# A hybrid encoder block with product-key expert retrieval on one core: reordered squares, table loads and gelus, narrower lookups, a shared gating product and another end

## Chip, cores and metric

The kernel runs on one core of one Trainium2 chip. The metric is the device time of one execution in microseconds (us); the median of three runs is given.

## What is computed

One layer on x of 512 tokens by 1024, all in float32. `peer` is where most of the time goes: each token picks 16 of 16384 experts for each of 8 heads, and the kernel computes it densely for three of the four blocks of 128 tokens and by gathering rows for the fourth.

```
h    = rms_norm(x, norm1_g)
u_a, v_a, q, k, v = split(h @ w_in)                       # 1024 -> 5 x 512
a_out = spatial_gating(gelu(u_a), gelu(v_a), ...)         # layer norm of v, 8 groups of 128x128
b_out = dilated_attention(rope(q), rope(k), v)            # windows (128,1), (512,4), (2048,16)
x    = x + concat(rms_norm(a_out), rms_norm(b_out)) @ w_out

# peer, on rms_norm(x, norm2_g), for each token and head:
s      = q @ sub_keys                                     # two lists of 128 scores
s1, i1 = top_k(s[0], 16);  s2, i2 = top_k(s[1], 16)
sc, ci = top_k((s1[:, None] + s2[None, :]).reshape(256), 16)
e      = i1[ci // 16] * 128 + i2[ci % 16]
g      = softmax(sc)
act    = gelu(xb @ expert_u[e].T)
x      = x + (g * act) @ expert_v[e]
out    = rms_norm(x, final_norm_g)
```

## The kernel before

The order of the work is written out by hand (`manual_schedule`): each engine does its instructions in the order in which the code issues them. TensorE multiplies float32 numbers as three products of split halves: `split` makes `hi` by a cast on ScalarE (L80) and `lo` by a subtraction on VectorE (L81) or, in some stages, GpSimd (L181), so that each weight tile costs a cast, a subtraction and three times the matmuls.

The stages, by the time of the profiled execution:

- Projections and attention, 0 to 240 us. `proj` multiplies x by pieces of w_in (matmuls L252) into five accumulators, four `acc` and one `pu`. The norm's factor is applied behind the product, so `xsq` makes the sums of squares of the four token blocks in `xss` during the first projection, `inv_root` makes `xrs` of them (a root on ScalarE, L146, and a reciprocal on VectorE), and the scaled copies of q (`qraw`, L270) empty the accumulators for the next projection. A function of ScalarE that its active table doesn't hold needs an ACT_TABLE_LOAD; `warm(f)` (L227) makes a tiny activation to have it early. v is emptied by gelus (`va`, L373).
- Query products and the choice of 16 out of 128, 241 to 346 us, then the rest of the routing up to 401 us: `top16` on VectorE, `decode`, `softmax`. `decode` turns the position ci of a chosen pair into two numbers of 0 to 15 (`rw`, `cl`) and looks the expert's indices up in the two lists: ScalarE spreads `rw` over 16 columns (`oh`, L681), VectorE compares with 0 to 15 (L688), multiplies by the list (L690), and adds the 16 columns pairwise (L695, L697). One call takes the three token blocks of three heads (n = 9 lists of 16 x 16 entries, 2304 numbers) or of two (n = 6). TensorE does the products with the first experts here (`ahead`, L201), up to AHEAD = 31 of 128.
- Gating, 401 to 541 us, 48 steps of 8 tokens. VectorE makes `ohb`, one-hot rows of the second and the first key (L855), and `oha`, the first key's one times the gate in two float16 halves, `gw` (L859); TensorE multiplies them, 16 matmuls of 128 columns (L896), which scatters the gates into a table of 128 x 128 for each token; ScalarE evacuates them into `wst` (`put`, L876), and DMAs on ScalarE's queue store it. `hots` runs two steps ahead of its matmuls. Between them stand 10 product matmuls of `ahead` a step with their casts (`uhi`, L170, and `ulo`, L181), and `flush` has ScalarE's gelus of finished products (`act`, L768).
- The main loop, 541 to 1479 us: e goes over 128 groups of 128 experts. Each e has 24 L201 matmuls (products with expert_u, for a later e, up to e = 96) and 18 L1041 matmuls (`vproduct`: three token blocks b, two halves n of 512 columns, three products hi hi, lo hi, hi lo, which add up in six accumulators over all e). Their inputs are `vhi`, `vlo` (`vsplit`) and `wahi`, `walo` (`wsplit`), for e + 1, made from `vraw`, loaded by SyncE's queue. In the same loop GpSimd gathers expert rows for the fourth token block, and VectorE takes dot products with them (L993) and adds them up (L1002); `rate` spreads these over the loop, and at e = NK - 3 those left are finished.
- The end: sums, gains and norms for the three dense blocks (`final_sum`, `gain`, `root`, `finish`), which begin when a block's accumulators are complete, and four stores.

## Time and profile before

| | |
|---|---|
| median of three runs | 1488.34 us (1487.87 to 1490.42) |
| profiled execution | 1490.96 us |
| its span | 1489.2 us |
| TensorE busy | 1453.4 us, 98% of the span |
| VectorE busy | 1159.6 us, 78% |
| ScalarE busy | 641.3 us, 43% |
| GpSimd busy | 283.6 us, 19% |
| granted TensorE clock, whole span | 0.996 |

The busy shares are means over stages with different limits. A stage has to be read from its own window, and a gap on TensorE from what ended it. PE is TensorE's matmul, PEld its weight load, DVE is VectorE, ACT is ScalarE, POOL is GpSimd, SPq and ACTq are the DMA queues of SyncE and ScalarE. A group xN in a timeline is N instructions in a row of one kind, and its length is the stretch that they take together; brackets give the idle time ahead and what ended it.

### The profile page before, as it was taken

The page shows a single profiled execution, that of the slowest core. Times are in us where ns is not written, and L with a number is a line of the kernel's source. Part 1 is how long each engine was busy: PE and PEld are TensorE (multiplying, and loading weights), DVE is VectorE, ACT ScalarE, POOL GpSimd, SP SyncE. Part 2 cuts the span into 40 slices and gives each one's busy share as a digit, 9 for nine tenths or more (in the row PEclk, how much of TensorE's full clock was granted, in tenths as well). Part 3 has the DMA queues.
Part 4 walks back from the last instruction along what each step waited for, and adds up shares of the span by engine and source line. Part 5 has one row for each costly group of instructions (what it writes and reads, how often), then busy time and mean ns, then how long its engine had stood idle before and what let it go on. Part 6 is the DMA issues. An engine that isn't in the chain of part 4 may idle for free.

```text
span 1489.2 us, 21574 instructions
## 1 busy us (share of the span) xinstructions
PE 1453.4 (98%) x7945; PEld 1292.6 (87%) x7945; DVE 1159.6 (78%) x2415; ACT 641.3 (43%) x1088; POOL 283.6 (19%) x222
## 2 busy tenths in 40 slices
PE   8999999999899999999999999999999999999997
PEld 6878988888888899999999999999999999987785
DVE  4745554999899967779878787888787888877775
ACT  5455753344555544434333333333333333323334
POOL 0040002445500000012222222222222222211002
PEclk9999999999999999999999999999999999999999
DMA  6331032232366776469999999999999998988764
GB/s 217 106 99 57 22 114 104 86 91 96 110 230 256 261 291 214 135 228 378 355 351 329 315 338 321 327 334 336 347 326 333 331 328 308 348 286 299 250 212 160
DMA packets 128777, 358.52 MB, mean 241 GB/s; under 512 B 9120, under 2 KB 59808, under 8 KB 112288
## 3 DMA queue, kind: packets, MB, share of 16 engines
q1 hardware_dynamic: 103184, 197.75, 40.1%
q0 software_dynamic: 18432, 134.23, 23.6%
q10 hardware_dynamic: 7056, 25.18, 4.2%
q8 instruction: 62, 1.02, 0.3%
q14 instruction: 43, 0.35, 0.1%
HBM read 327.10 MB, written 30.02 MB: 240 GB/s over the span
## 4 chain that ended last, share of the span: by engine, by line
PE 78%; DVE 9%; DMA 5%; issue 3%; ACT 3%; POOL 1%; ACTq 0%; SPq 0%; DVEq 0%; POOLq 0%
PE pu L201 34%; PE acc L1041 30%; PE acc L252 6%; DMA vraw<-in_uv_dram 3%; DVE ohb L855 3%; DVE oha L859 2%; DVE ulo L181 1%; DMA uraw<-in_uT_dram 1%; PE tr L734 1%; PE pu L252 1%; PE tr L434 1%; POOL ulo L181 1%; PE acc L447 1%; DVE vlo L81 1%; DMA xt<-in_x_dram 1%
## 5 line engine op out<-in xcount | busy, mean ns | idle before, releaser
L201 PE MATMUL pu<-h2T,uhi 128*128 128x384 f32 (+2 forms) x2336 | 451.0, 342 | 3.2 <-ACT act L768 2.4
L201 PEld LDWEIGHTS pu<-h2T,uhi 128*128 128x128 f32 x2336 | 409.6, 189 | 19.4 <-ACT act L768 3.1
L987 POOL DMA_INDIRECT uv<-in_uv_dram,ei x128 | 170.6, 1333 | 830.1 <-DVE xlast L1002 318.0
L81 DVE TENSOR_TENSOR vlo<-vraw,vhi 128x1024 fp32r<-128x1024 f32 x128 | 156.8, 1225 | 154.9 <-ACT vhi L80 154.7
L80 ACT CAST vhi<-vraw 128x1024 fp32r<-128x1024 f32 x128 | 134.6, 1051 | 296.3 <-issue 188.6
L1041 PE MATMUL acc<-vhi,wahi 128*128 128x512 f32 x768 | 238.7, 391 | 1.9 <-ACT wahi L80 1.9
L1041 PE MATMUL acc<-vlo,wahi 128*128 128x512 f32 x768 | 238.2, 391 | 0.5
L1041 PE MATMUL acc<-vhi,walo 128*128 128x512 f32 x768 | 237.8, 391 | 0.0
L201 PE MATMUL pu<-h2T,ulo 128*128 128x384 f32 (+2 forms) x1168 | 234.1, 340 | 2.3 <-POOL ulo L181 2.3
L201 PEld LDWEIGHTS pu<-h2T,ulo 128*128 128x128 f32 x1168 | 203.7, 188 | 7.4 <-POOL ulo L181 2.9
L170 ACT CAST uhi<-uraw 128x1024 fp32r<-128x1024 f32 x144 | 150.7, 1047 | 61.1 <-DMA uraw<-in_uT_dram 47.6
L1041 PEld LDWEIGHTS acc<-vlo,wahi 128*128 128x128 f32 x768 | 143.8, 188 | 33.7 <-DVE vlo L81 2.4
L1041 PEld LDWEIGHTS acc<-vhi,walo 128*128 128x128 f32 x768 | 143.7, 188 | 31.5 <-DVE walo L81 0.9
L1002 DVE SCALAR_TENSOR_TENSOR xlast<-uv,dot,xlast 128x1024 f32<-128x1024 f32 x128 | 164.5, 1285 | 4.5
L1041 PEld LDWEIGHTS acc<-vhi,wahi 128*128 128x128 f32 x768 | 142.6, 188 | 26.9 <-ACT wahi L80 3.1
L768 ACT ACTIVATE act<-pu 128x384 f32<-128x384 f32 x128 | 62.9, 492 | 234.9 <-PE pu L201 234.5
L993 DVE SCALAR_TENSOR_TENSOR uv<-uv,h 128x1024 f32<-128x1024 f32 x128 | 153.7, 1219 | 6.7 <-DMA uv<-in_uv_dram,ei 6.7
L181 DVE TENSOR_TENSOR ulo<-uraw,uhi 128x1024 fp32r<-128x1024 f32 x116 | 141.5, 1220 | 22.1 <-ACT uhi L170 21.9
L181 POOL TENSOR_TENSOR ulo<-uraw,uhi 128x512 fp32r<-128x512 f32 x56 | 81.5, 1479 | 209.4 <-ACT uhi L170 203.7
L81 DVE TENSOR_TENSOR walo<-wa,wahi 128x384 fp32r<-128x384 f32 x128 | 70.7, 553 | 0.6 <-ACT wahi L80 0.6
L80 ACT CAST wahi<-wa 128x384 fp32r<-128x384 f32 x128 | 65.2, 509 | 13.0 <-DVE wa L1026 12.9
L1026 DVE TENSOR_TENSOR wa<-act,wt 128x384 f32<-128x384 f32 x128 | 70.5, 551 | 0.0
(258 smaller groups left out, 1475.4 us busy)
## 6 DMA issues: line engine op xcount, KB each, us to landing
uraw<-in_uT_dram SPq DMA_DIRECT2D x128, 512.0 KB, 5.9
vraw<-in_uv_dram SPq DMA_DIRECT2D x128, 512.0 KB, 5.3
wd<-wst ACTq DMA_DIRECT2D x48, 512.0 KB, 3.1
wt<-wd SPq DMA_DIRECT2D x32, 768.0 KB, 10.6
wraw<-in_w_in_dram SPq DMA_DIRECT2D x19, 512.0 KB, 3.6
uraw<-in_w_q_dram SPq DMA_DIRECT2D x16, 512.0 KB, 3.8
xT<-in_xT_dram SPq DMA_DIRECT2D x8, 256.0 KB, 3.9
xt<-in_x_dram SPq DMA_DIRECT2D x1, 2048.0 KB, 11.5
```

The costliest lines, as they stand in the source:

```text
L80: S.copy(hi, src)
L81: sub.tensor_tensor(lo, src, hi.bitcast(F32), op=ALU.subtract)
L170: S.copy(hi, raws[i])
L181: eng.tensor_tensor(lo[:, k, :], raws[i][:, k, :], hi[:, k, :].bitcast(F32), op=ALU.subtract)
L201: T.matmul(o, l[:, k, :], r[:, k, t0:n], start=(p == 0 and k == 0), stop=(p == 2 and k == KT - 1))
L252: T.matmul(out[b], l[:, b * 128:(b + 1) * 128], r[:, kk, :], start=(k == 0 and i == 0), stop=(k == KT - 1 and i == 2))
L768: S.activation(acts[e], o[:, :DT], AF.Gelu_apprx_tanh)
L987: G.indirect_dma_start(out=uvs[r].rearrange("p s d -> p (s d)"), out_offset=None, in_=A["uv"], in_offset=bass.IndirectOffsetOnAxis(ap=ei[: ...
L993: V.scalar_tensor_tensor(uv[:, 0, :], uv[:, 0, :], 1.0, h2, op0=ALU.mult, op1=ALU.mult, accum_out=d[:, 0:1])
L1002: V.scalar_tensor_tensor(xlast, uv[:, 1, :], d[:, 1:2], xlast, op0=ALU.mult, op1=ALU.add)
L1026: eng.tensor_tensor(wa.rearrange("p (c t) -> p c t", c=NWC), acts.pop(e).rearrange("p (c t) -> p c t", c=NWC), wts[e // WG][:, :, e % WG, ...
L1041: T.matmul(acc[b][n], l[:, c], r[:, n * 512:(n + 1) * 512], start=(e == 0 and i == 0), stop=(e == NK - 1 and i == 2))
```

## The change

1. At the start `warm` loads the sqrt table in place of the one for Copy, and the squares of the odd token blocks are made on VectorE with an accumulating instruction.
2. The gelu table is loaded before the last head pair's casts of k, and the gelus of v go over the blocks in the order 1, 2, 3, 0.
3. `decode` looks up in 8 columns: 16 rows with the first 8 entries of a list and 8 rows (only those positions that can reach past 8) with the last 8, 192 numbers for a list in place of 256. The comparison table `iota_v` is made by GpSimd, once for each of the two pools.
4. In the gating stage VectorE makes `oha` for seven of eight tokens, and ScalarE the eighth's two halves, by copies scaled with a factor for each partition (`gs`), behind `flush`.
5. The gather's work is spread to end one expert earlier, and the rest is finished at e = NK - 4.
6. The split parts of the last two experts lie in the gather's buffers (`vl`, `wl`), so that those of the four last experts live side by side. Token block 2 of the last four experts (LASTV) is multiplied behind everything else, half n = 0 first, then n = 1.
7. Blocks 0 and 1 are finished with one product of sum, factor and gain on VectorE in halves; the last block's halves are scaled by VectorE and ScalarE and stored from two queues. GpSimd has no gains any more.

```diff
-    warm(AF.Copy)
+    warm(AF.Sqrt)
...
     def xsq(b):
         sq = tk.tile([128, 1024], F32, name="xs", bufs=4)
-        sumsq(sq, xt[:, b, :], xss[:, b:b + 1])
+        if b % 2:
+            V.scalar_tensor_tensor(sq, xt[:, b, :], 1.0, xt[:, b, :], op0=ALU.mult, op1=ALU.mult,
+                                   accum_out=xss[:, b:b + 1])
+        else:
+            sumsq(sq, xt[:, b, :], xss[:, b:b + 1])
...
-    for _ in range(4):
+    for p in range(4):
+        if p == 3:
+            warm(AF.Gelu_apprx_tanh)
         next(turning)
         drain(gen, 2)
-    warm(AF.Gelu_apprx_tanh)
...
-    for b in range(NB):
+    for b in (1, 2, 3, 0):
         S.activation(va[:, b, :], ps[b], AF.Gelu_apprx_tanh, scale=xrs[:, b:b + 1], accum_out=lns[:, 0, b:b + 1])
...
+    def lookup_rows(pool):
+
+        rows = pool.tile([128, 24, 8], BF16, name="iota_v")
+        for r0, r1, c0 in ((0, 16, 0), (16, 24, 8)):
+            G.tensor_copy(rows[:, r0:r1, :], iota[:, None, c0:c0 + 8].to_broadcast([128, r1 - r0, 8]))
+        return rows
...
         for r in (rw, cl):
-            oh = pool.tile([128, nh, nb, TOPK, TOPK], BF16, name="oh", bufs=3 if pool is rt else 2)
-            S.copy(oh.rearrange("p h b r c -> p (h b) r c"),
-                   r.rearrange("p h b k -> p (h b) k")[:, :, :, None].to_broadcast(wide))
+            oh = pool.tile([128, n, TOPK + K8, K8], BF16, name="oh", bufs=3 if pool is rt else 2)
+            flat = r.rearrange("p h b k -> p (h b) k")[:, :, :, None]
+            S.copy(oh[:, :, 0:TOPK, :], flat.to_broadcast([128, n, TOPK, K8]))
+            S.copy(oh[:, :, TOPK:, :], flat[:, :, K8:, :].to_broadcast([128, n, K8, K8]))
...
         for o in o4:
-            V.tensor_tensor(o, o, io, op=ALU.is_equal)
+            V.tensor_tensor(o, o, iota_v[:, None, :, :].to_broadcast([128, n, TOPK + K8, K8]), op=ALU.is_equal)
...
-        for w in (8, 4, 2):
+        for o in o4:
+            V.tensor_tensor(o[:, :, K8:TOPK, :], o[:, :, K8:TOPK, :], o[:, :, TOPK:, :], op=ALU.add)
+        for w in (4, 2):
...
-        wide = [128, 2, 8, NK // 2, 2]
-        V.tensor_tensor(a.rearrange("p (s t) (k two) -> p s t k two", s=2, two=2),
-                        c[:, None, 8:16].rearrange("p o t (k two) -> p o t k two", two=2).to_broadcast(wide),
-                        gw[:, g, :, :, None, :].to_broadcast(wide), op=ALU.mult)
+        wide = [128, 7, 2, NK // 2, 2]
+        V.tensor_tensor(a[:, 0:14].rearrange("p (t s) (k two) -> p t s k two", s=2, two=2),
+                        c[:, 8:15, None].rearrange("p t o (k two) -> p t o k two", two=2).to_broadcast(wide),
+                        gw[:, g, 0:7, :, None, :].to_broadcast(wide), op=ALU.mult)
+        rest.append((a, c, gs, g))
         return a, c
+
+    rest = []
+
+    def gated():
+        for a, c, gs, g in rest:
+            for s in range(2):
+                S.activation(a[:, 14 + s, :], c[:, 15, :], AF.Copy, scale=gs[:, g, s:s + 1])
+        rest.clear()
...
         put()
         flush()
+        gated()
...
-        if e < NK - 2:
-            for b in range(DB):
+        if e < NK - 1:
+            for b in range(DB if e < NK - LASTV else DB - 1):
                 vproduct(e, b)
...
+    lasts = range(NK - LASTV, NK)
+    for e in lasts:
+        vproduct(e, 2, (0,))
     for b in (0, 1):
-        finish(b, roots[b], eng=S)
-    vproduct(NK - 1, 2, (0,))
...
+        sums[b] = ex.tile([128, 2, 4], F32, name="ss", bufs=4)
+        sumsq(junk, xback[b], sums[b][:, 0, 0:1])
+        rs = inv_root(ex, sums[b][:, 0, 0:1], 1024)
+        for c in (slice(0, 512), slice(512, 1024)):
+            V.scalar_tensor_tensor(outs[b][:, c], xback[b][:, c], rs, fg[:, c], op0=ALU.mult, op1=ALU.mult)
+            Q.dma_start(out[b * 128:(b + 1) * 128, c], outs[b][:, c])
+        if b == 0:
+            final_sum(2, 0, 0, 512)
+    gain(2, 0, 512, V)
+    for e in lasts:
+        vproduct(e, 2, (1,))
+    for i, c0 in ((1, 512), (2, 768)):
+        final_sum(2, i, c0, c0 + 256)
     gain(2, 512, 1024, V)
-    finish(2, root(2, 3), (0, 512, 1024))
+    rs = root(2, 3)
+    V.tensor_scalar(xback[2][:, :512], outs[2][:, :512], rs, None, op0=ALU.mult)
+    S.activation(xback[2][:, 512:], outs[2][:, 512:], AF.Copy, scale=rs)
+    for q, c in ((Q, slice(0, 512)), (S, slice(512, 1024))):
+        q.dma_start(out[256:384, c], xback[2][:, c])
```

Where the order changes, three places matter. First ScalarE's row at the start, from the last of x's transposed parts (`thi`) to the scaled q; `xs` are the squares. Before:

```order
L80 CAST wph<-wraw 128x1024
L211 ACTIVATE thi<-xT,gains 128x512 x2
L151 ACTIVATE xs,xss<-xt 128x1024 x2
L80 CAST wph<-wraw 128x1024
L151 ACTIVATE xs,xss<-xt 128x1024 x2
L146 ACT_TABLE_LOAD
L146 ACTIVATE xrs<-xss,eps 128x4
L270 ACTIVATE qraw<-acc,xrs 128x512 x4
```

And in the changed kernel, where L152 is the same square and L147 the same root:

```order
L81 CAST wph<-wraw 128x1024
L212 ACTIVATE thi<-xT,gains 128x512 x2
L152 ACTIVATE xs,xss<-xt 128x1024
L81 CAST wph<-wraw 128x1024
L152 ACTIVATE xs,xss<-xt 128x1024
L147 ACTIVATE xrs<-xss,eps 128x4
L271 ACTIVATE qraw<-acc,xrs 128x512 x4
```

Two of the four squares and the table load have left the row.

Next ScalarE's row in the gating stage (`act` is a gelu, `wst` the evacuations, `uhi` a cast). Before:

```order
L768 ACTIVATE act<-pu 128x384
L876 ACTIVATE wst<-acc 128x128x4 x2
L170 CAST uhi<-uraw 128x1024
L876 ACTIVATE wst<-acc 128x128x4 x2
L768 ACTIVATE act<-pu 128x384
L884 DMA wd<-wst 128x1024
L876 ACTIVATE wst<-acc 128x128x4 x2
L884 DMA wd<-wst 128x1024
```

And now:

```order
L789 ACTIVATE act<-pu 128x384
L895 ACTIVATE oha<-ohb,gs 128x128 x2
L911 ACTIVATE wst<-acc 128x128x4 x2
L895 ACTIVATE oha<-ohb,gs 128x128 x2
L171 CAST uhi<-uraw 128x1024
L911 ACTIVATE wst<-acc 128x128x4 x2
L789 ACTIVATE act<-pu 128x384
L895 ACTIVATE oha<-ohb,gs 128x128 x2
L919 DMA wd<-wst 128x1024
```

Behind the gelu, or behind the evacuations where no gelu stands there, come the two scaled copies into `oha`, ahead of the next step's cast or evacuations.

Last ScalarE's row at the end, from the parts of the last but one expert on; `xlast` is the fourth token block, `fin` squares and scaled blocks. Before:

```order
L80 CAST vhi<-vraw 128x1024
L80 CAST wahi<-wa 128x384
L151 ACTIVATE fin,ss<-xlast 128x512 x2
L146 ACT_TABLE_LOAD
L146 ACTIVATE sd<-ss 128x1
L80 CAST vhi<-vraw 128x1024
L80 CAST wahi<-wa 128x384
L1106 ACTIVATE xlast<-h_5738,sd 128x1024
```

And now:

```order
L81 CAST vl<-vraw 128x1024
L81 CAST wl<-wa 128x384
L152 ACTIVATE fin,ss<-xlast 128x512 x2
L147 ACT_TABLE_LOAD
L147 ACTIVATE sd<-ss 128x1
L81 CAST vl<-vraw 128x1024
L81 CAST wl<-wa 128x384
L1155 ACTIVATE xlast<-h_5858,sd 128x1024
```

The casts of the last two experts keep their place behind the squares, the table load and the root of the fourth block; only their buffers differ. On TensorE the last twelve matmuls, which fill one accumulator with the half n = 1 of token block 2 of the last four experts, now read:

```order
L1090 MATMUL acc_5850<-vhi,wahi 128x512
L1090 MATMUL acc_5850<-vlo,wahi 128x512
L1090 MATMUL acc_5850<-vhi,walo 128x512
L1090 MATMUL acc_5850<-vhi,wahi 128x512
L1090 MATMUL acc_5850<-vlo,wahi 128x512
L1090 MATMUL acc_5850<-vhi,walo 128x512
L1090 MATMUL acc_5850<-vl,wl 128x512 x6
```

Before, the same rows held both accumulators of the last expert alone:

```order
L1041 MATMUL acc_5729<-vhi,walo 128x512
L1041 MATMUL acc_5730<-vhi,walo 128x512
L1041 MATMUL acc_5729<-vhi,wahi 128x512
L1041 MATMUL acc_5729<-vlo,wahi 128x512
L1041 MATMUL acc_5729<-vhi,walo 128x512
L1041 MATMUL acc_5730<-vhi,wahi 128x512
L1041 MATMUL acc_5730<-vlo,wahi 128x512
L1041 MATMUL acc_5730<-vhi,walo 128x512
```

So the last expert's parts are first read 36 matmuls before the end in the changed kernel, and 24 before.

## Rows read from the trace of the kernel before

**Rows 1.** TensorE's waits: total us, times, longest us
```profile
PE acc L896 <- DVE oha L859: 3.9, 10, 0.7
...
PE acc L1041 <- ACT wahi L80: 1.9, 3, 1.4
```

**Rows 2.** Windows: length, then each engine's busy us, granted clock, DMA share
```profile
25.00:50.00 25.00, 22.94 (x97) 18.16 (x96) 15.00 (x24) 13.36 (x21) 0.00 (x0) 0.93 0.23 64
350.00:375.00 25.00, 20.62 (x109) 19.98 (x108) 24.90 (x125) 12.34 (x13) 15.57 (x8) 0.93 0.26 88
401.00:536.00 135.00, 129.64 (x1211) 119.70 (x1210) 133.33 (x118) 79.46 (x138) 0.00 (x0) 1.00 0.65 242
```

**Rows 3.** Timeline of the start: start us, length, engine, instruction, idle before
```profile
24.35 1.06 ACT L151 ACTIVATE xs<-xt 128x1024 f32<-128x1024 f32 x1 [2.76 <-DMA xt<-in_x_dram]
...
29.59 1.28 ACT L146 ACT_TABLE_LOAD   x1
...
32.22 0.50 PE L252 MATMUL acc<-wph,thi 128*128 128x512 f32 x1 [2.06 <-ACT qraw L270]
...
33.89 0.63 PE L252 MATMUL acc<-wpl,thi 128*128 128x512 f32 x1
```

**Rows 4.** Timeline around the v gelus
```profile
81.47 1.28 ACT L227 ACT_TABLE_LOAD   x1
...
84.50 0.50 PE L252 MATMUL acc<-wph,thi 128*128 128x512 f32 x1 [1.34 <-ACT va L373]
```

**Rows 5.** Timeline of the routing, all engines
```profile
359.94 4.61 PE L201 MATMUL pu<-h2T,uhi 128*128 128x384 f32 x16 [2.38 <-ACT act L768]
...
365.06 2.63 DVE L688 TENSOR_TENSOR oh<-oh,iota_b 128x2304 bf16<-128x2304 bf16 x2
...
365.78 2.93 PE L201 MATMUL pu<-h2T,uhi 128*128 128x384 f32 x16
...
374.88 0.96 PE L201 MATMUL pu<-h2T,ulo 128*128 128x384 f32 x4 [2.00 <-POOL ulo L181]
...
386.85 0.96 DVE L688 TENSOR_TENSOR oh<-oh,iota_b 128x1536 bf16<-128x1536 bf16 x1 [1.42 <-ACT oh L681]
```

**Rows 6.** Groups by line, 401 to 536 us: busy us, mean ns, idle before
```profile
L859 DVE TENSOR_TENSOR oha<-ohb,gw 128x2048 f16<-128x2048 bf16 x47 | 57.6, 1225 | 1.6
...
L876 ACT ACTIVATE wst<-acc 128x512 f32<-128x512 f32 x92 | 50.0, 597 | 33.2 <-PE acc L896 32.9
...
L181 DVE TENSOR_TENSOR ulo<-uraw,uhi 128x1024 fp32r<-128x1024 f32 x19 | 23.2, 1219 | 0.0
L170 ACT CAST uhi<-uraw 128x1024 fp32r<-128x1024 f32 x20 | 21.0, 1051 | 8.0 <-PE pu L201 7.8
L768 ACT ACTIVATE act<-pu 128x384 f32<-128x384 f32 x20 | 9.9, 496 | 7.5 <-PE pu L201 7.1
```

**Rows 7.** Timeline of ScalarE in the gating stage, issue on its queue
```profile
436.05 0.33 ACTq L884 DMA_DIRECT2D wd<-wst  x1
```

**Rows 8.** Timeline of the end
```profile
1471.92 1.23 DVE L81 TENSOR_TENSOR vlo<-vraw,vhi 128x1024 fp32r<-128x1024 f32 x1 [0.32 <-ACT vhi L80]
...
1472.99 0.62 PE L1041 MATMUL acc<-vhi,wahi 128*128 128x512 f32 x2
...
1478.21 0.39 PE L1041 MATMUL acc<-vhi,walo 128*128 128x512 f32 x1
...
1484.70 0.88 DVE L1108 TENSOR_SCALAR fin<-fin,sd 128x512 f32<-128x512 f32 x2
```

**Rows 9.** Groups by line and shape, whole span: busy us, mean ns
```profile
L993 DVE SCALAR_TENSOR_TENSOR uv<-uv,h 128x1024 f32<-128x1024 f32 x128 | 153.7, 1219 | 6.7 <-DMA uv<-in_uv_dram,ei 6.7
...
L997 ACT ACTIVATE dot<-dot 128x1 f32<-128x1 f32 x128 | 21.9, 195 | 12.4 <-DVE uv L993 12.2
...
L270 ACT ACTIVATE qraw<-acc,xrs 128x512 f32<-128x512 f32 x7 | 4.3, 690 | 0.3 <-DVE xrs L147 0.3
```

**Rows 10.** The same view, 600 to 680 us
```profile
L695 DVE TENSOR_TENSOR oh<-oh 128x512 bf16<-128x512 bf16 x4 | 1.5, 419 | 0.0
```

More of the change, by code (lines that the diff above doesn't have):

```diff
@@ L946, in decoded @@
         def decoded(h):
-            return decode(gp, late[1][:, h:h + 4], gci[:, h:h + 4], [r[:, h:h + 4] for r in groute])
+            return decode(gp, iota_g, late[1][:, h:h + 4], gci[:, h:h + 4], [r[:, h:h + 4] for r in groute])
         for h in range(SOON, H):
@@ L1027, in wmul @@
                             acts.pop(e).rearrange("p (c t) -> p c t", c=NWC), wts[e // WG][:, :, e % WG, :], op=ALU.mult)
+    wlast = []
     def wsplit(e):
         if e in wmuls:
-            hi = ex.tile([128, DT], F32R, name="wahi")
-            lo = ex.tile([128, DT], F32R, name="walo")
+            if e < NK - 2:
+                hi = ex.tile([128, DT], F32R, name="wahi")
+                lo = ex.tile([128, DT], F32R, name="walo")
+            else:
+                if not wlast:
+                    wlast.append(ex.tile([128, 4, 512], F32R, name="wl", tag="uv", bufs=UVB))
+                hi, lo = (wlast[0][:, 2 * (e - NK + 2) + i, :DT] for i in range(2))
             split(hi, lo, wmuls.pop(e), V)
```

70 lines of the change are left out of this document (37 added, 33 removed).

## The prediction

> **What bounds the kernel now.** I read three views first. TensorE's waits come first [rows 1], because nothing that leaves TensorE's pace untouched can move the end of the main loop. They are short everywhere: 3.9 us on the one-hot product `oha` of the gating stage, 1.9 us on the cast `wahi`, and single waits that stand in the timelines below. Then the windows [rows 2] tell who is full in which stage. At 350 to 375 us VectorE is busy 24.90 of 25 us and TensorE 20.62. In the gating stage, 401 to 536 us, VectorE is busy 133.33 of 135 us and TensorE 129.64. So routing and gating are VectorE's, with TensorE only 5.4 us of idle time behind it, and the rest of the kernel, 541 to 1479 us, is TensorE's. At 25 to 50 us and at 350 to 375 us the granted clock is 0.93, and 1.00 in the gating stage: in two places TensorE fell from its 2.4 GHz level to the 1.2 GHz one. Last the timelines at the start, at the v gelus, at routing and at the end [rows 3, 4, 5, 8]. The time of the main loop itself, some 940 us, is the same matmuls in both kernels and I leave it out. The profiled execution took 1490.96 us, 2.6 more than the median of 1488.34; the terms below are differences inside the profiled one, and I take them off the median.
>
> **Start (edit: squares shared with VectorE, sqrt table loaded early).** Before, ScalarE makes the four squares of x itself, 1.05 us each from 24.35 on, and then loads the sqrt table at 29.59, 1.28 us; the scaled q follows at 31.48 and TensorE goes on at 32.22 after 2.06 us of idleness [rows 3]. The change removes that load from here (it takes the place of the Copy table's at the very start, so nothing is added) and moves two squares to VectorE, which waits there anyway. A square on VectorE is priced by the nearest row, the dot products of 1024 elements with an accumulator, 1.22 us plus a read of 0.08 (the 1219 ns of [rows 9]). ScalarE then does square, weight cast and square, 24.35 to 27.5; VectorE does square (24.35 to 25.65), the low part of the weights (26.5 to 27.7), square (27.8 to 29.1). The root follows at 29.1, then reciprocal and scaled q some 0.6 us later, and TensorE resumes near 30.4 instead of 32.22: 1.8 us. Behind the idle stretch the next matmuls stood at 0.63 us in place of 0.39, a pitch of 0.427 against 0.235 for eight of them (33.04 to 36.0, one of them in [rows 3]): 1.5 us. An idle stretch of 0.3 instead of 2.06 should not bring that; idle stretches of 1.34 and 2.00 in [rows 4, 5] were followed by matmuls at full pace. Together −3.3. If VectorE's second square is late and the clock falls all the same, −1.5; if the gap closes, −3.6.
>
> The Trainium skill, page "ScalarE: Activation LUTs", section "What ACT_TABLE_LOAD costs", puts a switch of tables at about 1.28 us and a drain of 1.38, 2.66 in all. The trace has the load at 1.28 and the root's activation 1.29 us after its start, with no second half, and the measurement decides; by the page the sum would be up to 1.4 us lower, to about 1473.8.
>
> **v gelus (edits: gelu table ahead of the last casts, b=1,2,3,0).** The table load stands at 81.47, behind the last casts, and TensorE waits 1.34 us until 84.50 for the first gelu that frees an accumulator it needs [rows 4]. The load goes ahead into ScalarE's idle time before these casts, and the accumulator which TensorE wants first is read first. The gelu of b=1 would start near 82.2 and release at 83.0, where TensorE's last matmul before the gap ends (83.16). −1.25; −0.6 if the load delays the casts by half.
>
> **Routing (edit: lookups of 8 and 16 entries).** From 319.5 to 386.8 VectorE has no idle time, so what it saves arrives one to one at the start of the gating stage. Its price per element comes from two rows: 2304 elements at a pitch of 1.31 us (two in 2.63, [rows 5]) and 512 elements at 0.419 [rows 10], so 0.50 ns per element and 0.15 us per instruction at most. A list of nine head-blocks shrinks from 2304 to 1728 elements: the compare saves 0.29 us, the product 0.29 less one more instruction (0.07 to 0.15), the first add 0.29 (1152 to 576 elements). For two lists 1.45 to 1.6; two such decodes and one of six head-blocks (two thirds, 0.85 to 1.0) make 3.8 to 4.2. ScalarE writes a quarter fewer entries, which shortens VectorE's idle 1.42 at 386.85 [rows 5] by 0.3 to 0.5. −4.5. The inner run falls from 16 to 8 elements; the 512-element add, whose run was 8, was at the full rate (0.419 = 0.15 + 512 × 0.5 ns), so I expect no loss. Lower bound −2: TensorE's own idle times here, 2.38 and 2.00 with a stretch of 16 matmuls in 4.61 instead of 2.93 us [rows 5], are then what stands next. Upper bound −8, where these shrink as well and the clock stays up. GpSimd's two small casts for the new table stand ahead of its `ulo` and hide, as it has idle time there.
>
> **Gating (edit: one token in eight on ScalarE).** The stage is 48 steps of `ohb` and `oha` on VectorE (1.22 each) with a `ulo` of 1.22 in every other step or so [rows 6]. `oha` shrinks from 2048 to 1792 elements: 256 × 0.5 ns × 48 = 6.1 us. The scalars `gs` add six instructions and `gw` is written in a strided way: +1.0. Net −5.1. TensorE's cover is 5.4 us in this stage [rows 2], so nearly all can be had: −5.0, range −2 to −5.4 (−6 with better waits). ScalarE gets two products of 128 elements a step. Their price isn't in the trace; it lies between the one-column activation with a pointer, 0.195, and the 512-column one, 0.690 [rows 9]; by the line between them 0.32. Evacuations take 50.0 us for 92, two a step 1.09; the 20 casts (21.0 us) and 20 activations (9.9) make 0.64 a step [rows 6], and the issue of a store, which isn't counted as busy, 0.33 [rows 7]. A step thus costs ScalarE 2.06 + 0.64 = 2.70 of the 2.75 us that the new step lasts (2.86 before, 137.5 us over 48), and some less where neighbours overlap, as the evacuations do (0.543 apart at 0.597 each). That is close. They stand behind `flush` and ahead of nothing urgent: TensorE reads them two steps later, at the last two of 16 matmuls. What queues behind them is the next evacuation, 0.6 late, and TensorE has four accumulators there, two steps' worth.
>
> The Trainium skill, same page and section, prices an activation at 186 ns and 0.833 ns per column with 93 ns more for each pointer operand, which would be 0.39 here. Its neighbours overlap by 93 ns there, so that two cost 0.59, a step would be 2.65 us, still under 2.75, and the sum would stay.
>
> **End (edits: block 2 of the last four experts last, other scaling).** The same matmuls run, at a pitch of 0.227 (24 from 1472.99 to 1478.4, [rows 8]). Block 2 of e=124 and 125, 12 matmuls, moves behind e=127's first ones, so these are wanted 2.72 us earlier, at 1470.27. Their inputs don't come earlier: ScalarE still has two squares of xlast, a table load and a root ahead of the last casts, and VectorE's `vlo` of the last expert runs from 1471.92 to 1473.15 [rows 8]. TensorE stalls there some 2.0 us. Behind the last matmul (1478.21) the old tail has sums, gains on GpSimd, and the two scalings, which end at 1485.58 (1484.70 + 0.88), 7.37 later [rows 8]. In the new one block 0 and 1 are finished with one product on VectorE each half, half of block 2 is summed before the last 12 matmuls, and the last scaling is shared by two engines and two queues: −1.1. Net +0.9. If vraw of the last expert comes early enough, −1.1; if the clock falls in the stall as at 32.22 and 359.94, +1.5 to 1.7 on top; so −1.1 to +3.5 with a DVE backlog. The finishing of gathers moved by an expert, and the parts of the last two experts in other buffers, cost nothing: TensorE's waits [rows 1] name no gather. TensorE's 1.9 us on `wahi` late in the loop [rows 1] comes from late vraw transfers; it can turn out 1.5 either way.
>
> **Sum:** −3.3 − 1.25 − 4.5 − 5.0 + 0.9 = −13.15. From the profiled 1490.96 that is 1477.8, and from the median 1475.2.
>
> **Rivals.** (1) ScalarE delays the evacuations and TensorE's reads, and most of the gating gain goes: 1475.2 + 4 = 1479. For it: 2.70 of 2.75 us. Against it: the products aren't wanted for two steps. 0.17. (2) The other side, slower: ScalarE becomes the bound of the gating stage. Its step is 2.06 us plus two products, so it passes VectorE's 2.75 from 0.35 us a product on. The rest of the sum (−8.15) is 0.17 us a step; the kernel gets slower than before once ScalarE's step is over 2.86 + 0.17 = 3.03, from 0.49 us a product on. At 0.6 it is 48 × (3.26 − 2.86) = +19, less 8: 1499.5. Only the row of 0.690 for 512 columns speaks for such a price; 0.03. (3) TensorE's clock falls in the stall at e=127: 1475.2 + 1.6 = 1476.8. 0.15. (4) The change doesn't do what it says: the short runs of 8 lose the rate and the lookups save nothing, or TensorE's waits in routing take it: D from −4.5 to +2, 1481.7. 0.08. (5) Better than forecast, since clock and waits in routing gain as well and the end has no stall: 1475.2 − 3.5 − 2.0 = 1469.7. 0.10. The forecast itself: 0.47.
>
> **Numbers.** Forecast 1475.2. The range takes in cases 1, 3, 4 and 5 with the bounds of the routing term: 1467.5 to 1483. A measurement of this kernel can tell about 0.2%, 3 us, from no change: faster means under 1485.3, slower over 1491.3. Only case 2 is beyond on the slow side, and a sum of all bad bounds (−1.5 − 0.6 − 2 − 2 + 3.5 + 1.5 = −1.1) lies in between: faster 0.92, same 0.05, slower 0.03.
>
> **What would show it.** At the start: no table load before the first root, TensorE's gap under 0.6, granted clock near 1.00 at 25 to 50 us. At 83 us: no wait for `va`. Routing: the gating stage's first `ohb` some 9 us earlier (with the two terms ahead). Gating: 48 steps in about 5 us less, ScalarE's products near 0.32 us, waits for `oha` of ScalarE under 2 us. End: a wait for `wl` or `vl` of 2 us in the last 10 us, and 6.3 us from the last matmul to the last scaling. I am wrong if TensorE waits for ScalarE in the gating stage by more than 4 us, or if the routing's VectorE chain isn't shorter by 3.8.

## The result

The changed kernel takes 1474.84 us (median, 1474.22 to 1475.35); the kernel before took 1489.0 us beside it (1487.28 to 1490.42). The ratio is 0.9905 with a 95% interval of 0.9893 to 0.9918. 1475.2 us had been forecast, faster by 13.15; it became faster by 14.2 us.

The page of the changed kernel has TensorE at the same share, and ScalarE with 98 instructions more:

```profile
span 1473.1 us, 21706 instructions
...
PE 1449.5 (98%) x7945; PEld 1291.3 (88%) x7945; DVE 1152.5 (78%) x2434; ACT 658.0 (45%) x1186; POOL 278.3 (19%) x222
```

The waits of TensorE that answer to [rows 1]: `oha` fell from 3.9 to 1.0 us, the wait for `wahi` is gone, and a new one, for `wl`, stands once.

```profile
PE acc L931 <- DVE oha L884: 1.0, 2, 0.8
PE acc L1090 <- ACT wl L81: 1.0, 1, 1.0
```

The windows that answer to [rows 2]. The gating stage begins near 393 us now, so its window is set at 390 to 525 us. In its middle, 430 to 450 us, TensorE is busy without a gap. In the kernel before, whose row stands last, it was idle for 1.15 of these 20 us:

```profile
25.00:50.00 25.00, 25.00 (x115) 20.23 (x114) 17.66 (x31) 11.40 (x19) 0.00 (x0) 1.00 0.34 104
390.00:525.00 135.00, 131.97 (x1242) 123.28 (x1242) 131.09 (x127) 105.01 (x235) 2.15 (x2) 1.00 0.66 244
430.00:450.00 20.00, 20.00 (x195) 18.66 (x194) 19.69 (x21) 15.28 (x35) 0.00 (x0) 1.00 0.70 263
```

```profile
430.00:450.00 20.00, 18.85 (x181) 17.73 (x182) 19.73 (x19) 13.68 (x26) 0.00 (x0) 1.00 0.68 248
```

Both kernels have 7945 matmuls in their traces, so the n-th matmul's start can be set against the n-th of before, as long as the order is the same, and at the very end as the last against the last. This lag is the shortest account of where the time went. Worked out from the starts in the traces (us, changed minus before):

| place | matmul | lag | forecast for the step |
|---|---|---|---|
| end of the first projection | 97 | +0.35 | |
| second projection | 300 | -3.48 | start -3.3 |
| third projection | 450 | -4.95 | v gelus -1.25 |
| query products | 1350 | -5.07 | |
| first gating matmuls | 2100 | -8.35 | routing -4.5 |
| main loop | 3450 to 7350 | -13.01 | gating -5.0 |
| e = 125 | 7900 | -16.43 | tail of the loop 0 |
| last matmul | 7944 | -14.69 | end, ahead of it: +2.0 |
| end of the span | | -16.1 | end, behind it: -1.1 |

So the start, the v gelus, gating and both parts of the end stand within 0.4 us of their forecast, routing is 1.2 us smaller, and 3.4 us in the tail of the loop were not forecast at all. These sum to 16.1 us between the two profiled executions, while the medians differ by 14.2: the profiled execution of before was a long one, by 2.0 us, and the experiments show where.

### The profile page after: what moved, and what is told of

Same layout as the page of the kernel before. It is cut to its first block, busy times and chain, and to the rows that moved or that the text cites. A ratio compares the mean times of both kernels' runs of the same rounds, so it can differ in the third digit from the quotient of the medians.

```text
span 1473.1 us, 21706 instructions
## 1 busy us (share of the span) xinstructions
PE 1449.5 (98%) x7945; PEld 1291.3 (88%) x7945; DVE 1152.5 (78%) x2434; ACT 658.0 (45%) x1186; POOL 278.3 (19%) x222
## 4 chain that ended last, share of the span: by engine, by line
PE 82%; DVE 11%; ACT 3%; issue 2%; DMA 1%; POOL 1%; ACTq 0%; SPq 0%; POOLq 0%; DVEq 0%
PE acc L1090 34%; PE pu L202 32%; PE acc L253 8%; DVE ohb L880 3%; DVE ulo L182 2%; DVE oha L884 2%; PE pu L253 1%; PE tr L440 1%; PE acc L453 1%; PE po L453 1%; DMA vraw<-in_uv_dram 1%; POOL ulo L182 1%; ACT uhi L171 1%; DMA uraw<-in_uT_dram 1%; PE pu L419 0%
## 5 line engine op out<-in xcount | busy, mean ns | idle before, releaser
L1090 PE MATMUL acc<-vhi,wahi 128*128 128x512 f32 x756 | 234.9, 391 | 0.0
L1090 PE MATMUL acc<-vlo,wahi 128*128 128x512 f32 x756 | 234.6, 391 | 0.0
L1090 PE MATMUL acc<-vhi,walo 128*128 128x512 f32 x756 | 234.2, 391 | 0.0
```

What stands on the lines that cost most here:

```text
L1090: T.matmul(acc[b][n], l[:, c], r[:, n * 512:(n + 1) * 512], start=(e == 0 and i == 0), stop=(e == NK - 1 and i == 2))
```

## The experiments

Eleven kernels were run, in three groups; each is compared with the kernel before on the same chip.

**Each edit by itself.** Four kernels have one part of the change each, on the kernel before. In the numbering of the section on the change, start_alone has its parts 1 and 2, lookups_alone part 3, gating_alone part 4, end_alone parts 5 to 7 (two of the expectations count otherwise and name the part in words). Of start_alone, lookups_alone, gating_alone and end_alone, in this order, the lines that mark the part:

```diff
-    warm(AF.Copy)
+    warm(AF.Sqrt)
...
-    for b in range(NB):
+    for b in (1, 2, 3, 0):
```

```diff
-        wide = [128, n, TOPK, TOPK]
...
+            oh = pool.tile([128, n, TOPK + K8, K8], BF16, name="oh", bufs=3 if pool is rt else 2)
```

```diff
-        wide = [128, 2, 8, NK // 2, 2]
+        wide = [128, 7, 2, NK // 2, 2]
...
+        gated()
```

```diff
+LASTV = 4
...
-                rate = 128.0 / ((NK - 5 - e) - (1.0 - SLOW) * RING)
+                rate = 128.0 / ((NK - 6 - e) - (1.0 - SLOW) * RING)
...
+            for b in range(DB if e < NK - LASTV else DB - 1):
```

> The kernel before with edits 1 and 2 alone (squares shared, sqrt and gelu tables earlier, v gelus in the order 1, 2, 3, 0). Theory: each stage's gain stands by itself, so TensorE is 3.5 us earlier from the second projection on and 5.0 us from the v gelus on, as in the changed kernel, and this reaches the end: -5.0 us against before. Rival: VectorE's routing swallows it, since VectorE, not TensorE, sets the start of the gating stage, and only what VectorE itself gets earlier counts: -2 us or less.

> The kernel before with edit 4 alone (lookups of 8 and 16 entries). Theory: VectorE's two large decodes and the small one get shorter by what their element counts say, less what GpSimd's subtraction at the same time takes back: -3.4 us, as the lag between the two traces showed over that stage. Rival of the element count alone: -4.5 us. Rival of the lost rate at runs of 8: 0 to +1 us.

> The kernel before with edit 3's counterpart in the gating stage alone (one token in eight gated by ScalarE). Theory: VectorE sets the pace of the 48 steps; -4.6 us, and each ScalarE product takes 0.40 us. Rival: ScalarE's queue sets it in part and the gain depends on the rest of the change: -2 us or less, with TensorE waiting for ScalarE's products or evacuations in the stage.

> The kernel before with the edits of the end alone (gather's work spread to end one expert earlier, parts of the last two experts in other buffers, block 2 of the last four experts last, other scaling). Theory A: the late waits for the parts of an expert in the tail of the loop, 3.4 us in the profile of before and none after, go by the gather's earlier end, and the end itself gives 1.4 behind the last matmul and takes 1.7 ahead of it: -1.5 to -3.5 us. Theory B: those waits come and go from run to run and the edit doesn't touch them: +0.3 us, and the profile still has waits for wahi of 1 to 3 us between 1323 and 1460 us.

| kernel | median | before | ratio, 95% interval | difference |
|---|---|---|---|---|
| start_alone | 1486.16 | 1488.74 | 0.9978, 0.9969 to 0.9988 | -2.6 |
| lookups_alone | 1484.40 | 1488.74 | 0.9968, 0.9956 to 0.9980 | -4.3 |
| gating_alone | 1483.77 | 1488.74 | 0.9969, 0.9958 to 0.9980 | -5.0 |
| end_alone | 1485.67 | 1488.74 | 0.9982, 0.9973 to 0.9991 | -3.1 |

The four differences sum to -15.0; the whole is -14.2. Each interval is some 1.5 us wide to either side, so the parts add up within what these runs can tell, about 3 us. lookups_alone's -4.3 can't separate its theory (-3.4) from the element count alone (-4.5); that the lookups would lose their rate (0 to +1) is ruled out, as is the rival of gating_alone (-2 or less). start_alone is off its forecast of -5.0, and by its median alone its rival (-2 or less) would stand. Its trace decides against the rival, since routing does not swallow the gain: in its trace TensorE is 5.5 us earlier than in the trace of before at the 450th matmul and still 5.8 at the 7350th, yet the median gained 2.6. Two things are in that gap.

The first is the start of before itself. No kernel but those with edit 1 changes anything ahead of the 300th matmul, so the other profiles are repetitions of the same start. x lands at another time in each, and ScalarE's first square and TensorE's idle time follow it. The rows of three of them, gating_alone, rate_alone and end_alone in this order: the first square, the first matmul behind the gap, and the window with the granted clock (the last number but two):

```profile
23.40 1.06 ACT L151 ACTIVATE xs<-xt 128x1024 f32<-128x1024 f32 x1 [2.97 <-DMA xt<-in_x_dram]
...
31.27 0.50 PE L252 MATMUL acc<-wph,thi 128*128 128x512 f32 x1 [0.29 <-ACT qraw L270]
```

```profile
25.00:50.00 25.00, 24.71 (x112) 19.71 (x111) 16.03 (x26) 13.55 (x21) 0.00 (x0) 1.00 0.29 89
```

```profile
23.92 1.06 ACT L151 ACTIVATE xs<-xt 128x1024 f32<-128x1024 f32 x1 [2.75 <-DMA xt<-in_x_dram]
```

```profile
31.80 0.50 PE L252 MATMUL acc<-wph,thi 128*128 128x512 f32 x1 [1.68 <-ACT qraw L270]
```

```profile
25.00:50.00 25.00, 23.32 (x106) 18.60 (x105) 15.69 (x25) 13.98 (x22) 0.00 (x0) 1.00 0.27 82
```

```profile
24.29 1.06 ACT L152 ACTIVATE xs<-xt 128x1024 f32<-128x1024 f32 x1 [3.21 <-DMA xt<-in_x_dram]
...
32.17 0.50 PE L253 MATMUL acc<-wph,thi 128*128 128x512 f32 x1 [2.00 <-ACT qraw L271]
```

```profile
25.00:50.00 25.00, 23.00 (x97) 18.15 (x96) 15.00 (x24) 13.33 (x22) 0.00 (x0) 0.93 0.23 71
```

First squares at 23.40, 23.92 and 24.29 us go with idle times of 0.29, 1.68 and 2.00 us; lookups_alone (24.04) has 1.20, and before, [rows 3], 24.35 and 2.06. So a later square mostly goes with a longer gap; lookups_alone is out of the order since TensorE itself was later there, by 0.6 us against rate_alone at the 97th matmul. TensorE's clock was granted in full behind 0.29, 1.20 and 1.68, and at 0.93 in the window behind 2.00 and 2.06. At the 300th matmul these five executions of the old order stand at 0, -0.1, -1.9, -2.0 and -2.5 us against the profiled one of before, -1.3 on the mean; the eight traces with the shared squares, seven of them with the early table too, stand at -3.5 to -4.1, -3.7 on the mean, however x lands. So against the mean of its executions the start is worth about 2.4 us, not 3.5.

The second is the tail of the loop, where start_alone waits for `wahi` 2.8 us in four places, more than the 1.9 of [rows 1], and its lag falls from -5.8 to -4.4. Whether the edit or chance made these waits longer stays open. end_alone speaks for its theory A: the long wait is gone there, two of 0.14 and 0.21 us for `wahi` are left (lag -2.2 at the 7900th matmul, from +0.1), and what the end itself takes and gives is small, +1.7 ahead of the last matmul and -1.4 behind it.

**The tail of the loop.** end_alone changes three things, so one number was changed alone on the kernel before (rate_alone), and set back alone in the changed kernel (rate_old):

```diff
-                rate = 128.0 / ((NK - 5 - e) - (1.0 - SLOW) * RING)
+                rate = 128.0 / ((NK - 6 - e) - (1.0 - SLOW) * RING)
```

> The changed kernel with the gather's old rate (spread to end at NK - 5 in place of NK - 6), all else as changed. In the four profiles with the old end, TensorE waits 1.3 to 1.8 us at the 7656th matmul and some 0.3 to 1.0 at two or three places 72 matmuls (four experts, one load of the gates' table wt) apart ahead of it; in the two with the new end these are gone. Theory A: the rate moves the gathers against these loads, so the waits come back here: +1.5 to +2.5 us against the changed kernel, -11.5 to -12.5 against before. Theory B: something else in the new end removes them (buffers, the order of SyncE's queue): no difference, -14 against before.

> The kernel before with one number changed: the gather is spread to end at NK - 6 in place of NK - 5. Theory A: this alone takes away the waits of TensorE in the tail of the loop (at the 7442nd to 7658th matmul), as putting the old rate back brought them back: -2 to -3 us against before, lag flat over these places. Rival: the waits need the rest of the new end too: no difference, and 1.3 to 1.8 us of waiting at the 7656th matmul.

rate_old took 1477.04 us (ratio to before 0.9924, 0.9911 to 0.9938), 2.2 more than the changed kernel; rate_alone 1484.79 against 1487.5 (0.9980, 0.9971 to 0.9989), 2.7 less than before. rate_alone is clear of no change; rate_old's interval touches the changed kernel's, and there the trace decides. Theory A holds both ways. In the trace of rate_old the lag behind the changed kernel grows by 3.4 us from the 7350th to the 7900th matmul; in that of rate_alone TensorE gains 4.3 on before there. That is all that before loses in this stretch: at four places, some 72 matmuls apart, its matmuls start further apart than the usual 0.227 us, by 4.3 us in all. Only 2.3 us of it is idle time, the rest are pairs that start 0.34 and 0.51 us apart around a wait. In rate_alone no two starts there lie over 0.3 us apart. The row that shows the mechanism is ScalarE's wait for the parts of an expert. In before, GpSimd's last gather is issued at 1400.28, 1.7 us behind a load of the gates' table, and the next vraw lands so late that ScalarE waits 6.45 us:

```profile
1398.56 0.43 SPq L1010 DMA_DIRECT2D wt<-wd  x1
...
1400.28 1.01 POOL L987 DMA_INDIRECT uv<-in_uv_dram,ei  x1 [9.04 <-DVE xlast L1002]
...
1401.65 12.09 SPq L1012 DMA_DIRECT2D vraw<-in_uv_dram  x3
...
1411.08 1.04 ACT L80 CAST vhi<-vraw 128x1024 fp32r<-128x1024 f32 x1 [6.45 <-DMA vraw<-in_uv_dram]
...
1412.59 0.73 PE L1041 MATMUL acc<-vhi,wahi 128*128 128x512 f32 x2 [1.45 <-ACT wahi L80]
```

In rate_alone no gather is issued any more near the same table load (the last one was at 1383.63), and the longest such wait of ScalarE behind that load is 2.5 us (from 1330 us to that load, beside gathers, up to 3.3):

```profile
1395.01 0.43 SPq L1010 DMA_DIRECT2D wt<-wd  x1
...
1397.85 11.74 SPq L1012 DMA_DIRECT2D vraw<-in_uv_dram  x4
...
1399.42 1.05 ACT L80 CAST vhi<-vraw 128x1024 fp32r<-128x1024 f32 x1 [2.50 <-DMA vraw<-in_uv_dram]
```

rate_old has its last gather again 1.7 us behind a table load (1384.10), and TensorE's long wait ends 12.0 us behind that gather, where before has 12.3:

```profile
1385.82 1.01 POOL L1025 DMA_INDIRECT uv<-in_uv_dram,ei  x1 [8.62 <-DVE xlast L1040]
...
1396.29 1.05 ACT L81 CAST vhi<-vraw 128x1024 fp32r<-128x1024 f32 x1 [6.06 <-DMA vraw<-in_uv_dram]
...
1397.80 0.73 PE L1090 MATMUL acc<-vhi,wahi 128*128 128x512 f32 x2 [1.06 <-ACT wahi L81]
```

The landing times in the trace of before say how the transfers meet. From 1000 us on, a vraw that is issued while neither a gather nor a table load is in flight lands 4.4 us later on the mean (12 of them), beside a gather 5.3 (37), beside a table load 5.2 (4), and beside both 6.9 (19); the one behind the last gather takes 9.3. rate_alone's trace gives 4.4, 5.3, 5.3 and 6.6. That the gather's rate makes the waits is shown by the two runs; that the transfers slow each other is read from these times, and what they share was not tried.

**The gating stage.** Two tokens of eight on ScalarE instead of one, six on VectorE (two_on_scalar, on the changed kernel):

```diff
-        wide = [128, 7, 2, NK // 2, 2]
+        wide = [128, 6, 2, NK // 2, 2]
...
-            for s in range(2):
-                S.activation(a[:, 14 + s, :], c[:, 15, :], AF.Copy, scale=gs[:, g, s:s + 1])
+            for t in range(2):
+                for s in range(2):
+                    S.activation(a[:, 12 + 2 * t + s, :], c[:, 14 + t, :], AF.Copy, scale=gs[:, g, t, s:s + 1])
```

> The changed kernel with two of eight tokens gated by ScalarE (four products of 128 columns a step) and six by VectorE. Theory (my rival 2 as a mechanism): a step of ScalarE is then 1.73 of evacuations, casts and gelus, 0.33 of store issue and four times 0.35 to 0.40, 3.5 to 3.7 us, over VectorE's 2.6: the stage gets longer by 48 x 0.7 to 0.9 = 33 to 43 us against the changed kernel, and TensorE waits for ScalarE. Rival: ScalarE's products overlap so well that VectorE still sets the pace: -6 us against the changed kernel.

1474.35 us (0.9911, 0.9896 to 0.9926): neither 33 us slower nor 6 faster, but the same. Both expectations fall. The groups of the changed kernel and of this one over the stage:

```profile
L884 DVE TENSOR_TENSOR oha<-ohb,gw 128x1792 f16<-128x1792 bf16 x48 | 52.4, 1092 | 1.6
L911 ACT ACTIVATE wst<-acc 128x512 f32<-128x512 f32 x96 | 51.7, 593 | 1.2 <-issue 0.6 <-DMA wd<-wst 0.6
...
L895 ACT ACTIVATE oha<-ohb,gs 128x128 f16<-128x128 bf16 x96 | 33.4, 400 | 27.8 <-DVE ohb L880 27.7
```

```profile
L896 ACT ACTIVATE oha<-ohb,gs 128x128 f16<-128x128 bf16 x190 | 63.9, 466 | 4.6 <-DVE ohb L880 4.6
...
L912 ACT ACTIVATE wst<-acc 128x512 f32<-128x512 f32 x92 | 52.5, 658 | 0.0
...
L884 DVE TENSOR_TENSOR oha<-ohb,gw 128x1536 f16<-128x1536 bf16 x48 | 46.0, 958 | 1.6
```

and the middle of the stage (busy us of TensorE, its weight loads, VectorE, ScalarE):

```profile
390.00:525.00 135.00, 132.10 (x1246) 123.99 (x1247) 127.04 (x128) 128.62 (x329) 1.37 (x2) 1.00 0.67 245
...
430.00:450.00 20.00, 20.00 (x200) 18.74 (x199) 19.69 (x22) 20.00 (x52) 0.00 (x0) 1.00 0.73 270
```

A product takes 0.400 us in the changed kernel, but the next starts 0.31 us after it (432.13 and 432.44, for one pair); 33.4 us for 96 make 0.35 each, and 63.9 us for 190, back to back more often, 0.34. The issue of a store does not add to the row: ScalarE's four products, evacuations, casts and gelus fill 128.6 of 135 us, which leaves no room for 0.33 us in each of the 48 steps, and in the changed kernel an activation starts inside 42 of the 48 issues. VectorE's row shrinks to 127.0 us, and yet the stage keeps its length: from the 2130th to the 3340th matmul it lasts 136.7 us before, 131.6 in the changed kernel and 131.3 here. TensorE is busy 20.00 of 20 us in both, but in two_on_scalar ScalarE is too, so the matmuls' starts have to decide which of them is the bound. Between these two matmuls the starts of neighbours of one kind lie as far apart in all three kernels (at the median 0.056 us for the gating products, 0.174 for those of `ahead`). What differs is the step from `ahead` to the gating products: over the usual 0.18 us, the 43 such steps lose 6.7 us together before, 1.3 in the changed kernel and 0.0 in two_on_scalar. So TensorE's matmuls follow each other at their own pace, and TensorE is the bound of the stage as soon as one token in eight is gone from VectorE's row.

**The table load at the start.** The changed kernel with the old table first (copy_table):

```diff
-    warm(AF.Sqrt)
+    warm(AF.Copy)
```

> The changed kernel with the table of Copy loaded at the start as before, so that the sqrt table (1.28 us) is loaded ahead of the first root again; the squares stay shared. Theory: TensorE's gap ahead of the second projection is 0.3 us in the changed kernel and becomes 1.3 to 1.6 us; the gaps of 0.29 and 1.20 us in two profiles of the old order kept the clock, those of 2.00 and 2.06 lost it, so here the clock stays and the cost is the load alone: +1.2 us against the changed kernel, -12.8 against before. Rival: the clock falls here too: +2.7 us, granted clock 0.93 at 25 to 50 us.

1476.05 us (0.9918, 0.9904 to 0.9931), from 1474.29 to 1477.55, against 1474.22 to 1475.35. The median is 1.2 above, as expected, but the intervals overlap and the profile can't bear it out: in it x landed early (first square at 22.24), the load was over at 28.55 and TensorE had no idle time ahead of the second projection. So in this execution, with the squares shared, the load cost nothing. What it costs where x lands late, and how the gain of the start divides between squares and table, is not shown.

**The end.** Three kernels on the changed one. root_late puts the fourth block's root behind the last casts:

```diff
-        if e == NK - 3:
+        if e == NK - 2:
             outs[gb] = h2
```

end_reordered has this, and block 2's first sum behind block 1's scaling:

```diff
-        if b == 0:
-            final_sum(2, 0, 0, 512)
+    final_sum(2, 0, 0, 512)
     gain(2, 0, 512, V)
```

end_spread has root_late's move, both squares ahead of block 2's sum, block 1's halves (`give` is the product and its store) ahead of and behind the last sums, one gain on GpSimd, and the sums of squares added up ahead of the last gain:

```diff
+    final_sum(2, 0, 0, 512)
+    gain(2, 0, 512, G)
+    give(1, lo_half)
     for e in lasts:
         vproduct(e, 2, (1,))
     for i, c0 in ((1, 512), (2, 768)):
         final_sum(2, i, c0, c0 + 256)
+    give(1, hi_half)
```

> The changed kernel with two moves in the end: the fourth block's squares, table load and root stand behind the last expert's casts on ScalarE (at e = NK - 2 in place of NK - 3), and the sum of block 2's first half stands behind block 1's square and scaling. Theory: the 0.97 us wait for wl of the last expert and the slower pair behind it go (-1.4 us), and VectorE, which reached the last sums 2.4 us after the last matmul since block 1's square stood on ScalarE behind a square of block 2, is there when the last matmul ends (-2.0 us): -3 us or more against the changed kernel, some 1471.5 us. Rival: the vraw of the last expert lands too late anyway (issued behind the split of the expert before it), so that only the second part comes: -1.5 to -2 us.

> The changed kernel with the fourth block's squares, table load and root behind the last expert's casts on ScalarE (at e = NK - 2 in place of NK - 3), nothing else moved. Theory: the wait for wl of the last expert, 0.97 us, and the slow pair behind it go: -1.4 us against the changed kernel on TensorE, and less at the end, since VectorE reaches the last sums late for another reason: -0.3 to -1.4 us, 1473.5 to 1474.5. Rival: the wait is the transfer of vraw and stays.

> The reordered end (fourth block's root late) with VectorE's work behind the last matmul cut further: GpSimd makes the gain of block 2's first half, and block 1's scaled halves stand before and behind the last sums, so that VectorE reaches these some 0.7 us earlier. Theory: the end is VectorE's row from the last matmul on, so each 0.7 us taken off it counts: -0.5 to -1.0 us against the reordered end, 1472 us. Rival: GpSimd's gain, 1.8 us, comes late or slows VectorE's instructions beside it: no gain or a loss of up to 1 us.

| kernel | median | ratio to before, 95% interval | last matmul to end of span |
|---|---|---|---|
| changed kernel | 1474.84 | 0.9905, 0.9893 to 0.9918 | 9.6 |
| root_late | 1474.25 | 0.9906, 0.9891 to 0.9921 | 10.9 |
| end_reordered | 1472.74 | 0.9895, 0.9880 to 0.9910 | 8.6 |
| end_spread | 1470.35 | 0.9882, 0.9866 to 0.9897 | 7.5 |

The medians of the first three lie within each other's intervals, so the account of the end rests on the traces. root_late takes the wait away on TensorE: between the 7900th and the last matmul it gains 1.6 us on the changed kernel, so its rival, a wait for the transfer, falls. But the end comes 1.3 us later behind the last matmul, so that little is left. The row that shows it is VectorE's last sums (L1130), which start when VectorE gets to them, in the changed kernel and in root_late:

```profile
1455.02 3.44 PE L1090 MATMUL acc<-vl,wl 128*128 128x512 f32 x12 [0.97 <-ACT wl L81]
...
1462.38 1.52 PE L1090 MATMUL acc<-vl,wl 128*128 128x512 f32 x6
...
1462.70 1.06 ACT L152 ACTIVATE fin<-fin 128x1024 f32<-128x1024 f32 x1
...
1464.41 1.42 DVE L1234 SCALAR_TENSOR_TENSOR fin<-fin,sd 128x512 f32<-128x512 f32 x2
...
1466.34 0.75 DVE L1130 TENSOR_TENSOR fin<-acc,fin 128x256 f32<-128x256 f32 x2
...
1468.78 0.49 DVE L1245 TENSOR_SCALAR fin<-fin,sd 128x512 f32<-128x512 f32 x1
```

```profile
1461.81 1.06 ACT L152 ACTIVATE fin<-fin 128x1024 f32<-128x1024 f32 x1
...
1463.52 1.42 DVE L1234 SCALAR_TENSOR_TENSOR fin<-fin,sd 128x512 f32<-128x512 f32 x2
...
1465.45 0.75 DVE L1130 TENSOR_TENSOR fin<-acc,fin 128x256 f32<-128x256 f32 x2
```

The last matmul ends near 1463.9 and 1461.7 there, and the sums wait 2.4 and 3.7 us for block 1's scaling, whose square stands on ScalarE behind a square of block 2 that needs a matmul's end. In end_reordered TensorE gains 1.7 us there, more than the 1.4 expected, and the end 1.1 behind it, for 2.0; its median, 1472.74, is 2.1 below the changed kernel's, for 3. In end_spread the sums come at once:

```profile
1458.58 1.05 ACT L152 ACTIVATE fin<-fin 128x1024 f32<-128x1024 f32 x1
...
1461.06 1.71 POOL L1141 TENSOR_TENSOR fin<-fin 128x512 f32<-128x512 f32 x1 [21.36 <-DVE fin L1130]
...
1461.77 0.76 DVE L1130 TENSOR_TENSOR fin<-acc,fin 128x256 f32<-128x256 f32 x2
...
1464.44 0.49 DVE L1257 TENSOR_SCALAR fin<-fin,sd 128x512 f32<-128x512 f32 x1
```

end_spread is faster than before by 17.2 us (in its own group: 1487.5 to 1470.35), and its median is 4.5 below the changed kernel's and below the 1472 expected. Its interval and that of the changed kernel overlap, so the 4.5 is not sure by the medians; the traces hold 4.3 of it, TensorE's last matmul 2.2 us earlier (0.5 of it gained ahead of the 7900th) and the end 2.2 us sooner behind it.

## Why the prediction was right, step by step

The forecast of 1475.2 was met within 0.4 us, partly by errors that cancel.

**Start, in the trace right, against the median too large.** The trace gave -3.48 for -3.3; the gap closed, for the 0.3 us worked out, and the clock stayed up as forecast. ScalarE's and VectorE's rows came as laid out; x landed 0.5 us earlier here (first square at 23.86), and the root stands at 28.78 for 29.1:

```profile
26.19 1.05 ACT L152 ACTIVATE xs<-xt 128x1024 f32<-128x1024 f32 x1
...
27.46 1.22 DVE L313 SCALAR_TENSOR_TENSOR xs<-xt 128x1024 f32<-128x1024 f32 x1
...
28.78 0.30 ACT L147 ACTIVATE xrs<-xss,eps 128x4 f32<-128x4 f32 x1 [1.45 <-DVE xs L313]
...
29.38 2.42 ACT L271 ACTIVATE qraw<-acc,xrs 128x512 f32<-128x512 f32 x4 [0.30 <-PE acc L253]
```

The step that failed is the carrying over: the term was a difference to one execution whose idle time of 2.06 us and fallen clock three of the five profiled executions of the same code don't have. About 2.4 us would have been right, for 3.3.

**v gelus, right.** -1.47 for -1.25; the wait for `va` in [rows 4] is gone.

**Routing, mis-sized.** -3.3 in the changed kernel and -3.2 in lookups_alone (lag -1.87 to -5.09), for -4.5; between the same matmuls six other traces with the edit show -3.4 to -4.0. VectorE's row, from the first instruction of `top16` to the gating stage's first `ohb`, takes 145.0 to 145.3 us in the five kernels without the edit and 141.2 to 142.1 in the eight with it. In the changed kernel it is shorter by 3.1, under the 3.8 that the prediction gave as a sign of being wrong. The price per element was right: 1728 elements took 1.046 us on the mean, for 0.15 + 1728 × 0.5 ns = 1.01, and the rival of the lost rate falls. What failed is that the saved time arrives whole. In the changed kernel four adds of 576 elements took 0.987 us on the mean, against 0.448 in lookups_alone:

```profile
L702 DVE TENSOR_TENSOR oh<-oh,iota_v 128x1728 bf16<-128x1728 bf16 x4 | 4.0, 1046 | 0.0
L711 DVE TENSOR_TENSOR oh<-oh 128x576 bf16<-128x576 bf16 x4 | 3.8, 987 | 0.0
```

```profile
L705 DVE TENSOR_TENSOR oh<-oh 128x576 bf16<-128x576 bf16 x4 | 1.6, 448 | 0.0
```

Two of the four lasted 1.50 and 1.54 us, the other two 0.45. The two long ones stand beside the halves of a subtraction on GpSimd:

```profile
328.54 2.75 POOL L182 TENSOR_TENSOR ulo<-uraw,uhi 128x512 fp32r<-128x512 f32 x2 [3.29 <-ACT uhi L171]
328.64 2.96 DVE L711 TENSOR_TENSOR oh<-oh 128x576 bf16<-128x576 bf16 x2
```

So it is with all of them. In that row 12 instructions before, 13 in lookups_alone and 14 in the changed kernel last at least 0.4 us longer than the shortest of their shape in any run. Each overlaps GpSimd's subtractions for about half of its length or more, and together they are longer by 11.8, 13.8 and 14.6 us. Without this excess the lookups' own instructions take 26.2 us before and 21.9 in both other kernels: 4.3 saved, for the 3.8 to 4.2 forecast. Some 2 to 3 us of it are lost again to the further stretching. That GpSimd's subtraction stretches them is read from these overlaps; no run moved it.

**Gating, right in size, and for the reason given as its limit.** -4.7 for -5.0, between the lags at the 2100th and the 3450th matmul. The prediction put TensorE's cover at 5.4 us; the stage got shorter by 5.1, and TensorE is busy without a gap in its middle. Two prices behind it were off and cost nothing: a product took 0.400 us, not 0.32, and a store's issue is not part of ScalarE's row. By the Trainium skill, page "ScalarE: Activation LUTs", section "What ACT_TABLE_LOAD costs", an activation takes 186 ns and 0.833 ns a column, each pointer operand adds about 93 ns, and neighbours overlap by about 93 ns; an estimate from these figures is 0.39 us for 128 columns with one pointer operand, and 0.29 from one start to the next. The trace's 0.400 and the 0.31 between neighbours agree with that, and it was a better price than the line drawn between two rows. The rival of a ScalarE-bound stage, with 0.35 us a product as its point, was wrong in its own arithmetic: with four products, twice the load, the stage did not get longer.

**Tail of the loop, wrong.** The step was "The finishing of gathers moved by an expert [...] cost nothing: TensorE's waits [rows 1] name no gather". It gained 3.4 us between the profiled executions, and rate_alone's 2.7 shows that the changed rate does it. The wait names the cast that TensorE waits for, and the prediction stopped there. It gave the wait as a spread of 1.5 either way, and left the gather out, which stands two steps behind it: cast, transfer, and the transfers beside that one. It also took the 1.9 us of the wait for the loss; with the slow pairs around the waits the loss in that execution was 4.3.

**End, right.** TensorE lost 1.7 us (lag from -16.43 to -14.69), for 2.0, at the wait for `wl` that was named: 1.0 of it idle, the rest slower pairs around it. Behind the last matmul 1.4 were gained, for 1.1: together +0.4 for +0.9. The clock stayed up. That the 1.4 were so few has the reason that root_late and end_spread show: VectorE's row, not the matmuls, sets the end.

Sum, by the sizes that the runs give the steps: 2.4 (start), 1.5, 3.3, 4.7 and 2.7 (tail), less 0.4 (end), 14.2 us, as measured; so close a match is partly luck, as rate_alone's 2.7 is itself known only to about 1.4. Against the forecast 0.9 was too much at the start, 1.2 in routing and 0.3 in gating; 0.2 and 0.5 too little at the v gelus and the end, and 2.7 in the tail not seen: 1.0 more than forecast in all. That the time was met within 0.4 has a second piece of luck in it: the median of before moved up by 0.7 between the two groups of runs (1488.34 to 1489.0).

## What to carry to other kernels

Before a gap in one profiled execution is priced, look whether it depends on when a transfer lands: then its worth against the median is a mean over executions, and every profile of a kernel that leaves this stretch alone is one more sample of it. A stage in which the second engine is busy 96% of the time gives back only the rest, whatever is taken from the first; the next edit there has to go to the second. A wait put down to a cast deserves the question what the cast waited for, and what else was moving then: here one number in a rate was worth 2.7 us, nearly as much as the rewritten lookups' 3.3. And an engine's saved time arrives only as far as no other engine's work stands beside what is left: VectorE saved what its elements said, and lost part of it again beside GpSimd.
